# Chunked recurrence of the even layer: three chunk inverses side by side, a ring of half banks, a late norm in four spans

## The chip, the cores and the metric

The kernel runs on one core of a Trainium2 chip. The metric is the device time of one execution in microseconds: 2305.53 us, the median of three runs (2305.34 to 2306.35). One more execution was profiled; all rows below come from that one.

## The reference, cut to what matters

The kernel computes one step of a two-layer decoder trunk for 536 tokens: 16 meta tokens and 512 prompt tokens as one sequence, and 8 single sample tokens with states of their own. Each layer is a half SwiGLU block, a mixer, and a second half SwiGLU block. The change is in the mixer of the even layer, which runs HGRN2 heads (4) and RWKV-7 heads (8 of width 64) in parallel. RWKV-7 is a recurrence over tokens:

```
def rwkv7_scan(r, w, k, v, kk, a, s0):
    def step(s, inp):
        rt, wt, kt, vt, kkt, at = inp
        sa = jnp.einsum('bhij,bhj->bhi', s, -kkt)
        s = s * wt[:, :, None, :] + sa[..., None] * (kkt * at)[:, :, None, :] + vt[..., None] * kt[:, :, None, :]
        y = jnp.einsum('bhij,bhj->bhi', s, rt)
        return s, y
...
    mu = jnp.mean(y, axis=-1, keepdims=True)
    var = jnp.mean(jnp.square(y - mu), axis=-1, keepdims=True)
    yn = ((y - mu) * lax.rsqrt(var + RWKV_GN_EPS)).reshape(bsz, t, B_W) * prm['rwkv_ln_w'][e] + prm['rwkv_ln_b'][e]
    bonus = jnp.sum(r4 * k4 * prm['rwkv_rk'][e].reshape(B_HEADS, B_N), axis=-1, keepdims=True) * v4
    ob = (yn + bonus.reshape(bsz, t, B_W)) * g
    mix = jnp.concatenate([oa.astype(f32), ob], axis=-1).astype(h.dtype) @ prm['even_w_out'][e]
```

`oa` is the normalized output of the HGRN heads. The norm of `y` over each head, the bonus and the gate `g` are called the late norm here (`rpost`).

## The kernel before, in words

All activations lie transposed: 128 channels on the partitions, 536 tokens along the free dimension. Dense products run as three fp32r matmuls (high by high, high by low, low by high), in token parts of 272 and 264 columns (`PARTS`); a projection of 128 channels is 8 x 3 x 536 = 12,864 columns, and the program counts TensorE work in such columns.

The prompt's recurrence runs in chunks: one of 16 tokens and eight of 64, for two halves `d` of four heads each (two pairs of heads per half). That makes 18 chunks. For a chunk, `stage_g` (lines 1136 to 1172) spreads the rows over a block-diagonal tile, multiplies and transposes; then a unit triangular matrix is inverted by doubling, in up to five levels of two steps. `lev_t` (1175 to 1190) multiplies into `t1` (L1182), transposes the running inverse `xx` from the second level on (L1187), and ScalarE copies both out of PSUM (L1188, L1190). `lev_x` (1192 to 1206) multiplies again (L1204, L1198) and VectorE copies the result under a mask into `xx` (L1206, L1199). These 11 steps (7 for the short chunk) are a chain in which each step needs the one before. Five output steps follow, which also need the state of the chunk before: `st_p`, `st_t`, `st_sa`, `st_s`, `st_y` (1209 to 1264). All of them take PSUM from the ring `w`, four banks, one bank per request.

`waves` (1121 to 1302) puts these 280 steps into a list of slots: the two halves `d` are two chains, each chunk's inverse following that of the chunk before, and a chunk's output steps lie in the five slots behind its inverse. `even_mixer` (its loop is in the print below) calls one step after the other and puts filler between them. TensorE's queue is in the order in which the program is written (`manual_schedule`); the other engines are ordered by the framework's scheduler. After each step the loop adds `FILL` columns of credit, up to `FILL_MAX`, and spends it on `th_`: HGRN's projections (`proj_steps`, L240 to L242) and its heads' cores, `hcore` with `gla_core` and `gla_step` (scores L627, L638 and L618, factors L646, L657 on VectorE and L658 on GpSimd, state and output L669 to L713, sample states L724 to L752). Once these are used up it takes `mo`, the output projection of the first token part (`mix_out`), if two marks are set: "first" (HGRN's norm, `hgrn_norm`, is done) and "half" (the late norm has passed token 272).

Every `SAMPLE_EVERY`-th step advances `ts`, the sample's RWKV-7 step (`rsample`, four pairs of heads one after the other: transposes L1069, a trip through DRAM to broadcast the rows, products on GpSimd L1091 to L1115, reductions on VectorE L1094 and L1117). It works in the buffers `acc` and `sq`, of which there is one each; HGRN's norm and the late norm use the same two. Every `POST_EVERY`-th step advances `po`, which waits until head 3 of HGRN is projected and the recurrence has passed the end of the span, draws the rest of `ts`, lets HGRN's norm run if the heads are done, and then runs the late norm `rpost` over one span of tokens (`SPANS`) for two pairs of heads at a time. When the last step is issued, the loop issues what is left of `th_`, then of `po`, with `mo` between as the marks allow, then the rest of `mo`.

Of the kernel before, what the change touches and what calls it, by code (L numbers as in the profile page):

```python
# [63 lines left out]
LAG, LAG_LATER = 2, 3  # L64
SMALL_BLOCK = 32

HEAD_EVERY, ODD_FILL = 5, 4000
# [39 lines left out]
def trunk(ctx, tc, A, O):  # L107
    nc = tc.nc
# [15 lines left out]
    def psum(**sizes):  # L124
        if sizes == {tag: n for tag, (_, n) in rings.items()}:
            return
        banks.close()
        rings.clear()
        for tag, n in sizes.items():
            pool = banks.enter_context(tc.tile_pool(name=f"ps{tag}", bufs=n, space=bass.MemoryType.PSUM))  # L130
            rings[tag] = (pool, n)

    def bank(tag="m"):
        return til(rings[tag][0], [P, 512], tag)


    cf = til(cst, [P, CF_RM], "cf")
# [983 lines left out]
    def waves(pool, R):  # L1121
# [13 lines left out]

        def stage_g(d, ci, U):
            t0, n = CHUNKS[ci]
            na, nl = (2, 32) if n == 64 else (1, n)

            def both(z):  # L1140
                return z.rearrange("p (a h l) -> p a h l", a=2, h=2)[:, :na, :, :nl]

            U["xx"] = til(pool, [P, 2, 256], "xx", bufs=3)
            U["gm"] = til(pool, [P, 2, 320], "gm", bufs=3)
            nc.scalar.copy(U["xx"].rearrange("p u (v c) -> p (u v) c", v=2), ident.unsqueeze(1).to_broadcast([P, 4, P]))
            U["tm"] = til(pool, [P, 2, 384], "tm", bufs=3)
            if n < 64:
                nc.gpsimd.memset(U["gm"], 0.0)
            for i in range(2):
                Q = R[2 * d + i]  # L1150
                b_ = bd[i]
                for h in range(2):
                    hs = slice(64 * h, 64 * h + 64)
                    dst = b_[hs].rearrange("p (v a h l) -> p v a h l", v=4, a=2, h=2)[:, :, :na, h, :nl]
                    nc.vector.tensor_copy(dst, Q["sl"][hs, 0:4, t0:t0 + n].rearrange("p v (a l) -> p v a l", l=nl))
                g = bank("w")
                gv = g[:, 128:384].rearrange("p (v w t) -> p v w t", v=2, w=2)
                rhs = Q["sl"][:, 3:5, t0:t0 + n]
                nc.tensor.matmul(g[:, 0:128], b_[:, 384:512], b_[:, 0:128], start=True, stop=True)
                nc.tensor.matmul(gv[:, 0, :, :n], b_[:, 0:128], rhs, start=True, stop=True)  # L1160
                nc.tensor.matmul(gv[:, 1, :, :n], b_[:, 128:256], rhs, start=True, stop=True)
                one = g[:, 128:128 + n].rearrange("p (a l) -> p a l", l=nl)
                nc.vector.tensor_mul(both(U["gm"][:, i, 0:128]), one.unsqueeze(2).to_broadcast([P, na, 2, nl]),
                                     both(maskg[:, 0:128]))
                nc.vector.copy_predicated(U["xx"][:, i, 0:128], cu[:, CU_R:CU_R + 128], g[:, 0:128])
                nc.vector.tensor_mul(*(z.rearrange("p (v t) -> p v t", v=3)[:, :, :n]
                                       for z in (U["gm"][:, i, 128:320], g[:, 192:384], maskg[:, 128:320])))
                pt = bank("w")
                for v in range(3):
                    nc.tensor.transpose(pt[:, 128 * v:128 * v + 128], b_[:, 128 * v:128 * v + 128], ident)  # L1170
                nc.scalar.copy(U["tm"][:, i], pt[:, :384])
            nc.vector.copy_predicated(U["xx"][:, :, 128:256], lmask(0)[:, :, 128:256], U["gm"][:, :, 0:128])


        def lev_t(U, li):
            pt = bank("w")
            U["t1"] = til(pool, [P, 2, P], "t1", bufs=2)

            rs, cs = (slice(64, 128), slice(0, 64)) if li == 5 else (slice(0, 128), slice(0, 128))
            ks = cs  # L1180
            for i in range(2):
                nc.tensor.matmul(pt[rs, 128 * i:128 * i + cs.stop], U["gm"][ks, i, rs], U["xx"][ks, i, cs],  # L1182
                                 start=True, stop=True)
            if li > 1:
                px = bank("w")
                for i in range(2):
                    nc.tensor.transpose(px[:, 128 * i:128 * i + 128], U["xx"][:, i, 0:128], ident)  # L1187
            nc.scalar.copy(U["t1"][rs, :, cs], pt[rs, 0:256].rearrange("p (u c) -> p u c", u=2)[:, :, cs])  # L1188
            if li > 1:
                nc.scalar.copy(U["xx"][:, :, 128:256], px[:, 0:256].rearrange("p (u c) -> p u c", u=2))  # L1190
# [35 lines left out]
        def st_t(d, ci, U):  # L1226
            pt = bank("w")
            for i in range(2):
                nc.tensor.transpose(pt[:, 128 * i:128 * i + 128], pd[d][:, i], ident)
            U["pp"] = til(pool, [P, 2, P], "pp", bufs=2)  # L1230
            nc.scalar.copy(U["pp"], pt[:, 0:256].rearrange("p (u c) -> p u c", u=2))

        def st_sa(d, ci, U):
            ps = bank("w")
            for i in range(2):
                nc.tensor.matmul(ps[:, 128 * i:128 * i + 128], U["xx"][:, i, 128:256], U["pp"][:, i],
                                 start=True, stop=True)
            U["sa"] = til(pool, [P, 2, P], "sa", bufs=2)
            nc.scalar.copy(U["sa"], ps[:, 0:256].rearrange("p (u c) -> p u c", u=2))

        def st_s(d, ci, U):
# [52 lines left out]
        for d in range(2):  # L1294
            for i in range(2):
                p = 2 * d + i
                ps = bank("w")
                nc.tensor.transpose(ps[:, :P], S[d][:, i], ident)
                so = til(pool, [P, 64], "so", bufs=2)
# [393 lines left out]
```

## Time and profile before

| | |
|---|---|
| median of three runs | 2305.53 us |
| profiled execution, own time | 2313.27 us |
| profiled execution, span | 2311.5 us |
| mean granted TensorE clock | 0.991 of full speed |
| TensorE busy | 2256.8 us, 98% |
| VectorE busy | 1646.7 us, 71% |
| ScalarE busy | 1082.8 us, 47% |
| GpSimd busy | 143.5 us, 6% |
| HBM | 98 GB/s over the span |

PE is TensorE, DVE VectorE, ACT ScalarE, POOL GpSimd, SP the queue that issues most DMAs. Busy time counts an engine as busy while any of its instructions runs; matmuls overlap, so their single durations (about 0.28 us) are longer than the distance between their starts. An fp32 matmul of the recurrence shows as two records. The chunked recurrence runs from about 516 to 865 us of the span; the late norm's last span and the output projection follow.

### The profile page before, as it was taken

What the parts mean: (1) busy time and instruction counts of PE and PEld (TensorE: products, weight loads), DVE (VectorE), ACT (ScalarE), POOL (GpSimd) and SP (SyncE); (2) the same over time, 40 slices, a digit from 0 to 9 for tenths busy, and PEclk for the clock granted to TensorE, in tenths of its full rate; (3) what the DMA queues carried; (4) which work ended last, traced back from release to release, by engine and by line L of the source; (5) the groups of instructions that cost most, each with busy time, mean ns of one, the idle gap of its engine ahead of it and who ended that gap; (6) DMA issues with size and microseconds to landing.
All of it is one profiled execution on the core that took longest, in us unless ns stands there. A gap on an engine that the chain in (4) does not pass through costs nothing.

```text
span 2311.5 us, 47443 instructions
## 1 busy us (share of the span) xinstructions
PE 2256.8 (98%) x19520; PEld 2206.5 (95%) x19520; DVE 1646.7 (71%) x2971; ACT 1082.8 (47%) x2056; POOL 143.5 (6%) x192
## 2 busy tenths in 40 slices
PE   8999999999999999999999999999999999999998
PEld 8999999998998888999999999999999889999998
DVE  7858576686666878966757885857666777948576
ACT  6525254374444456434535452525434464525355
POOL 0000000312212100000000000000021210000000
PEclk9999999999999999999999999999999999999999
DMA  6323334223222116242423332333434353333324
GB/s 171 106 78 101 92 92 132 81 64 94 79 71 72 49 49 167 74 119 75 118 74 101 92 110 74 101 92 94 128 110 128 111 160 92 92 92 101 110 85 136
DMA packets 409393, 229.23 MB, mean 99 GB/s; under 512 B 19252, under 2 KB 400501, under 8 KB 409176
## 3 DMA queue, kind: packets, MB, share of 16 engines
q1 hardware_dynamic: 408456, 224.78, 33.5%
q8 instruction: 153, 2.51, 0.5%
q10 hardware_dynamic: 720, 1.42, 0.2%
q14 instruction: 64, 0.52, 0.1%
HBM read 211.19 MB, written 14.97 MB: 98 GB/s over the span
## 4 chain that ended last, share of the span: by engine, by line
PE 86%; DVE 5%; DMA 3%; ACT 2%; issue 1%; POOL 1%; SPq 0%; ACTq 0%; POOLq 0%; DVEq 0%
PE d L334 21%; PE d L335 21%; PE d L336 21%; PE d L240 5%; PE d L242 4%; PE d L241 4%; PE w L1182 1%; PE w L1204 1%; DMA vb<-dv 1%; DVE wlo L229 1%; DMA raw<-in_even_w_out_dram 1%; PE m L155 1%; DMA sq<-dr 1%; DMA raw<-in_odd_w_out_dram 1%; PE w L1187 1%
## 5 line engine op out<-in xcount | busy, mean ns | idle before, releaser
L240 PE MATMUL d<-hh,whi 128*128 128x264 f32 (+2 forms) x1136 | 343.6, 303 | 2.0 <-DVE xT L596 1.3
L242 PE MATMUL d<-hh,wlo 128*128 128x264 f32 (+2 forms) x1136 | 326.7, 288 | 1.9 <-DVE wlo L229 1.7
L241 PE MATMUL d<-hl,whi 128*128 128x264 f32 (+2 forms) x1136 | 326.6, 288 | 0.5 <-DVE hl L1418 0.5
L334 PE MATMUL d<-hh,whi 128*128 128x268 f32 (+1 forms) x832 | 237.8, 286 | 1.8 <-ACT hh L187 1.3
L335 PE MATMUL d<-hl,whi 128*128 128x268 f32 (+1 forms) x832 | 238.1, 286 | 0.9 <-DVE hl L188 0.9
L336 PE MATMUL d<-hh,wlo 128*128 128x268 f32 (+1 forms) x832 | 237.7, 286 | 0.7 <-DVE wlo L293 0.7
L240 PEld LDWEIGHTS d<-hh,whi 128*128 128x128 f32 x1136 | 216.1, 190 | 7.5 <-issue 2.4
L242 PEld LDWEIGHTS d<-hh,wlo 128*128 128x128 f32 x1136 | 215.4, 190 | 4.6 <-DVE wlo L229 4.0
L241 PEld LDWEIGHTS d<-hl,whi 128*128 128x128 f32 x1136 | 216.3, 190 | 0.9 <-DVE hl L1418 0.7
L534 DVE SCALAR_TENSOR_TENSOR xT<-d,xT 128x272 f32<-128x272 f32 (+2 forms) x192 | 82.9, 433 | 166.7 <-PE d L336 166.6
L334 PE MATMUL d<-hid,whi 128*128 128x264 f32 (+2 forms) x704 | 201.5, 287 | 0.0
L334 PE MATMUL d<-hid,whix 128*128 128x264 f32 (+2 forms) x704 | 201.2, 286 | 0.0
L335 PE MATMUL d<-hid,whix 128*128 128x264 f32 (+2 forms) x704 | 200.8, 285 | 0.0
L335 PE MATMUL d<-hid,whi 128*128 128x264 f32 (+2 forms) x704 | 200.7, 286 | 0.0
L336 PE MATMUL d<-hid,wlox 128*128 128x264 f32 (+2 forms) x704 | 200.6, 285 | 0.0
L336 PE MATMUL d<-hid,wlo 128*128 128x264 f32 (+2 forms) x704 | 200.5, 286 | 0.0
L334 PE MATMUL d<-sumh,whix 128*128 128x268 f32 (+1 forms) x576 | 170.9, 297 | 0.0
L336 PE MATMUL d<-sumh,wlo 128*128 128x268 f32 (+1 forms) x576 | 164.7, 286 | 0.0
L335 PE MATMUL d<-suml,whix 128*128 128x268 f32 (+1 forms) x576 | 164.4, 285 | 0.0
L334 PE MATMUL d<-sumh,whi 128*128 128x268 f32 (+1 forms) x576 | 164.2, 285 | 0.0
L336 PE MATMUL d<-sumh,wlox 128*128 128x268 f32 (+1 forms) x576 | 164.0, 285 | 0.0
L335 PE MATMUL d<-suml,whi 128*128 128x268 f32 (+1 forms) x576 | 164.0, 285 | 0.0
(383 smaller groups left out, 6557.8 us busy)
## 6 DMA issues: line engine op xcount, KB each, us to landing
raw<-in_ffn_gate_dram SPq DMA_DIRECT2D x44, 512.0 KB
raw<-in_ffn_up_dram SPq DMA_DIRECT2D x44, 512.0 KB
rawx<-in_ffn_gate_dram SPq DMA_DIRECT2D x44, 512.0 KB
rawx<-in_ffn_up_dram SPq DMA_DIRECT2D x44, 512.0 KB
raw<-in_ffn_down_dram SPq DMA_DIRECT2D x32, 512.0 KB
rawx<-in_ffn_down_dram SPq DMA_DIRECT2D x32, 512.0 KB
raw<-in_even_w_in_dram SPq DMA_DIRECT2D x30, 512.0 KB
raw<-in_odd_w_in_dram SPq DMA_DIRECT2D x25, 512.0 KB
```

What stands on the lines that cost most here:

```text
L155: nc.tensor.matmul(ps[:, :b - a], lhsT, rhs[:, a:b], start=True, stop=True)
L229: nc.vector.tensor_sub(lo[:, ks], raw[:, ks], hi[:, ks].bitcast(F32))
L240: nc.tensor.matmul(o, hi[:, k], h, start=(k == 0), stop=False)
L241: nc.tensor.matmul(o, hi[:, k], l, start=False, stop=False)
L242: nc.tensor.matmul(o, lo[:, k], h, start=False, stop=(k == nk - 1))
L334: nc.tensor.matmul(o, hi[:, k], rh(k), start=start and k == 0, stop=False, **kw)
L335: nc.tensor.matmul(o, hi[:, k], rl(k), start=False, stop=False, **kw)
L336: nc.tensor.matmul(o, lo[:, k], rh(k), start=False, stop=stop and k == nk - 1, **kw)
L534: nc.vector.scalar_tensor_tensor(xv[:, sl], ps, -0.5, xv[:, sl], ALU.mult, ALU.add)
L1182: nc.tensor.matmul(pt[rs, 128 * i:128 * i + cs.stop], U["gm"][ks, i, rs], U["xx"][ks, i, cs], start=True, stop=True)
L1187: nc.tensor.transpose(px[:, 128 * i:128 * i + 128], U["xx"][:, i, 0:128], ident)
L1204: nc.tensor.matmul(pd[:, i], lhsT, rhs, start=True, stop=True)
```

## The change

Five things change, all in the even layer.

- `waves` has `CHAINS` = 3 chains instead of two. The 18 chunks are dealt to whichever chain is free first, the halves `d` taking turns; a chain's steps are three slots apart, its start is staggered by four slots, and a chunk's output steps are two slots apart (`OUT_STEP`).
- The ring `w` still has four banks, but a request now gets half a bank of 256 columns (`halves`); two requests in a row share one bank. `stage_g` is cut to fit: its products take two halves, its transposes one and a half, and ScalarE copies them in two pieces.
- The late norm has four spans instead of three, since 272 columns don't fit a half bank.
- `FILL` is 550 instead of 1100, `SAMPLE_EVERY` 6 instead of 3, `POST_EVERY` 5 instead of 3.
- Buffer counts: `xx`, `gm`, `tm` 4 instead of 3, `t1` 3 instead of 2, `pp`, `sa` and `so` 1 instead of 2.

```diff
-FILL, FILL_MAX = 1100, 5000
+FILL, FILL_MAX = 550, 5000
...
-SAMPLE_EVERY, POST_EVERY = 3, 3
-SPANS = [0, 272, 400, 536]
-LAG, LAG_LATER = 2, 3
+SAMPLE_EVERY, POST_EVERY = 6, 5
+SPANS = [0, 144, 272, 400, 536]
+
+
+CHAINS, STAGGER, OUT_STEP = 3, 4, 2
...
     def bank(tag="m"):
-        return til(rings[tag][0], [P, 512], tag)
+        if tag != "w":
+            return til(rings[tag][0], [P, 512], tag)
+
+        if not halves:
+            t = til(rings[tag][0], [P, 512], tag)
+            halves.extend((t[:, 256:512], t[:, 0:256]))
+        return halves.pop()
...
-                g = bank("w")
-                gv = g[:, 128:384].rearrange("p (v w t) -> p v w t", v=2, w=2)
+                g, gl = bank("w"), bank("w")
+                gv = g.rearrange("p (v w t) -> p v w t", v=2, w=2)
...
+                nc.tensor.transpose(gl[:, 128:256], b_[:, 0:128], ident)
                 pt = bank("w")
-                for v in range(3):
-                    nc.tensor.transpose(pt[:, 128 * v:128 * v + 128], b_[:, 128 * v:128 * v + 128], ident)
-                nc.scalar.copy(U["tm"][:, i], pt[:, :384])
+                for v in range(2):
+                    nc.tensor.transpose(pt[:, 128 * v:128 * v + 128], b_[:, 128 * v + 128:128 * v + 256], ident)
+                nc.scalar.copy(U["tm"][:, i, 0:128], gl[:, 128:256])
+                nc.scalar.copy(U["tm"][:, i, 128:384], pt)
...
         slots = {}
-        for d in range(2):
-            t = LAG * d
-            for w in range(9):
-                U = {}
-                for fn in inverse(d, w, U):
-                    slots.setdefault(t, []).append((1 + d, fn, 0))
-                    t += 1
-                if w == 0 and d == 1:
-                    t += LAG_LATER
-                for i, st in enumerate((st_p, st_t, st_sa, st_s, st_y)):
-                    fn = lambda st=st, d=d, w=w, U=U: st(d, w, U)
-                    slots.setdefault(t + i, []).append((0, fn, int(i == 4)))
+        free = [STAGGER * i for i in range(CHAINS)]
+        after, ends = [0, 0], []
+        for c in range(18):
+            d, w, U = c % 2, c // 2, {}
+            k = free.index(min(free))
+            t = max(free[k], ends[c - CHAINS - 1] if c > CHAINS else 0)
+            for fn in inverse(d, w, U):
+                slots.setdefault(t, []).append((1 + k, fn, 0))
+                t += CHAINS
+            free[k] = t
+            t = max(t - CHAINS + 2, after[d])
+            for i, st in enumerate((st_p, st_t, st_sa, st_s, st_y)):
+                fn = lambda st=st, d=d, w=w, U=U: st(d, w, U)
+                slots.setdefault(t + OUT_STEP * i, []).append((0, fn, int(i == 4)))
+            after[d] = t + 4 * OUT_STEP
+            ends.append(after[d])
```

The order of instructions on TensorE, in the middle of the recurrence, with the semaphores that an instruction waits for. Before: two products of `lev_x` (L1204) of two chains, each with a ring tile `w` of its own, and three projection matmuls.

```order
L1204 MATMUL w_7519<-t_1124_7459,xx_7377 128x128 [waits Activation_49]
L1204 MATMUL w_7519<-t_1124_7459,xx_7377 128x128
L1204 MATMUL w_7523<-t_1126_7467,xx_7062 128x128 [waits Activation_49]
L1204 MATMUL w_7523<-t_1126_7467,xx_7062 128x128
L240 MATMUL d_7373<-hh_70,whi_7154 128x264
L241 MATMUL d_7373<-hl_71,whi_7154 128x264
L242 MATMUL d_7373<-hh_70,wlo_7155 128x264
```

After, the same step (now L1217) of two chains; both write the ring tile w_6679.

```order
L1217 MATMUL w_6679<-t_936_6652,xx_6420 128x128 [waits PE_49]
L1217 MATMUL w_6679<-t_936_6652,xx_6420 128x128
L251 MATMUL d_6462<-hh_70,whi_6130 128x264
L252 MATMUL d_6462<-hl_71,whi_6130 128x264
L253 MATMUL d_6462<-hh_70,wlo_6131 128x264
L1217 MATMUL w_6679<-t_938_6660,xx_6566 128x128 [waits DVE_49,Activation_49]
L1217 MATMUL w_6679<-t_938_6660,xx_6566 128x128
```

The end of the recurrence after the change: the four transposes of the last states (L1298 before, L1315 now) take two tiles, two transposes each, ahead of HGRN's scores.

```order
L251 MATMUL d_9234<-hh_70,whi_9227 128x272
L252 MATMUL d_9234<-hl_71,whi_9227 128x272
L253 MATMUL d_9234<-hh_70,wlo_9228 128x272
L1315 MATMUL w_9338<-cf_66,S_1430_9249 128x128 [waits PE_49]
L1315 MATMUL w_9338<-cf_66,S_1430_9249 128x128 [waits Activation_49]
L1315 MATMUL w_9349<-cf_66,S_1443_9324 128x128 [waits PE_49]
L1315 MATMUL w_9349<-cf_66,S_1443_9324 128x128 [waits Activation_49]
```

The second of the two transposes that share a tile now carries a wait for ScalarE, which copies the first one out.

TensorE again, the transposes and the state of HGRN's head 3. Before, they lie between chain steps (L1204, L1182, L1187, L1261) and the late norm (L155 on `w`).

```order
L155 MATMUL w_9869<-sl_616_4518,cf_66 128x272
L1204 MATMUL w_9873<-t_1624_9831,xx_9355 128x128 x2
L669 MATMUL m_9878<-cf_66,hk_8793 128x128 x4
L675 MATMUL m_9885<-cf_66,hv_9103 128x128 x4
L679 MATMUL m_9892<-cf_66,hk_8793 16x128
L681 MATMUL m_9892<-cf_66,hv_9103 16x128
L1182 MATMUL w_9896<-xx_9711,gm_9712 128x128 x2
L1187 MATMUL w_9900<-cf_66,xx_9711 128x128 x2
L688 MATMUL m_9906<-mtm_9891 128x128
L695 MATMUL m_9909<-vt_9884,ktm_9877 128x128 x4
L1261 MATMUL w_9923<-gm_9144,sa_9820 128x64 x2
L155 MATMUL w_9930<-lg_4507,g_604_4506 128x272
```

After, head 3's core stands behind the last step of the recurrence; here its last outputs (L723, L724), the transposes of the sample's last pair (L1080), the sum of HGRN's norm (L166 on `m`) and the first late norm (L166 on `w`).

```order
L724 MATMUL m_10068<-hq_9225,S_10058 128x128
L723 MATMUL m_10068<-acc_9807,vt_10035 128x128
L724 MATMUL m_10068<-hq_9225,S_10060 128x128
L1080 MATMUL m_10085<-cf_66,sl_616_4518 8x128
L1080 MATMUL m_10085<-cf_66,ws_618_4520 8x128
L1080 MATMUL m_10085<-cf_66,sl_616_4518 8x128 x2
L1080 MATMUL m_10094<-cf_66,sl_616_4518 8x128
L166 MATMUL m_10139<-acc_10127,cf_66 128x272
L166 MATMUL m_10143<-acc_10127,cf_66 128x264
L166 MATMUL w_10160<-sl_607_4509,cf_66 128x144
L166 MATMUL w_10160<-sl_610_4512,cf_66 128x144
L166 MATMUL w_10167<-acc_10159,cf_66 128x144
```

No chain step and no projection matmul stands between these any more.

## Rows read from the trace of the kernel before

**Rows 1.** Page: span, and busy time of TensorE with its share.

```profile
span 2311.5 us, 47443 instructions
PE 2256.8 (98%) x19520; PEld 2206.5 (95%) x19520; DVE 1646.7 (71%) x2971; ACT 1082.8 (47%) x2056; POOL 143.5 (6%) x192
```

**Rows 2.** Stretches: length, busy PE, PEld, DVE, ACT, POOL (counts), PEclk, DMA share, GB/s.

```profile
516.00:865.00 349.00, 329.73 (x3414) 308.04 (x3412) 245.39 (x709) 161.33 (x436) 71.45 (x78) 0.98 0.24 68
```

**Rows 3.** Waits of PE, 516 to 865: us in total, times, longest.

```profile
PE w L1182 <- DVE xx L1206: 2.3, 4, 0.9
```

**Rows 4.** Timeline of PE, projection matmuls: start, us, engine, instruction.

```profile
589.02 0.28 PE L240 MATMUL d<-hh,whi 128*128 128x272 f32 x1
589.15 0.29 PE L241 MATMUL d<-hl,whi 128*128 128x272 f32 x1
```

**Rows 5.** Timeline: level product, VectorE's copy, next product (idle before in brackets).

```profile
839.72 0.61 PE L1204 MATMUL w<-t,xx 128*128 128x128 f32 x4
840.53 0.38 DVE L1206 COPY_PREDICATED xx<-cu,w 128x256 f32<-128x256 uint8 x1
...
840.97 0.71 PE L1182 MATMUL w<-xx,gm 128*128 128x128 f32 x4 [0.64 <-DVE xx L1206]
```

**Rows 6.** Timeline: head 3 of HGRN, first, one level, last.

```profile
777.51 0.27 PE L724 MATMUL m<-cf,hv 128*8 128x128 f32 x1
...
781.13 0.46 PE L627 MATMUL m<-hq,hk 128*32 128x32 f32 x32
...
781.67 0.30 DVE L632 COPY_PREDICATED accd<-cu,m 128x128 f32<-128x128 uint8 x1
...
781.81 0.86 POOL L658 TENSOR_TENSOR hk<-hk,hf 128x264 f32<-128x264 f32 x1 [39.76 <-DVE xx L1206]
...
781.96 1.00 DVE L657 TENSOR_TENSOR hq<-hq,hf 128x264 f32<-128x264 f32 x1
...
816.39 0.39 PE L713 MATMUL m<-hq,S 128*128 128x128 f32 x2
```

**Rows 7.** Timeline: sample, second pair (first three) and last pair.

```profile
586.00 0.27 PE L1069 MATMUL m<-cf,sl 128*8 128x128 f32 x1
...
597.22 1.28 POOL L1091 TENSOR_TENSOR sq<-acc,sq 128x512 f32<-128x512 f32 x1 [33.65 <-DMA acc<-in_state_rwkv_dram]
...
625.95 0.69 DVE L1117 TENSOR_REDUCE sl<-sq 128x8 f32<-128x512 f32 x1 [2.79 <-POOL sq L1115]
...
716.36 1.47 POOL L1091 TENSOR_TENSOR sq<-acc,sq 128x512 f32<-128x512 f32 x1
...
740.78 1.27 POOL L1115 TENSOR_TENSOR sq<-acc,sq 128x512 f32<-128x512 f32 x1 [4.27 <-DMA sq<-dr]
```

**Rows 8.** Groups by line: HGRN's norm (829 to 848), late norm (865 to 890): busy, mean ns.

```profile
L179 ACT ACTIVATE sq<-oa 128x536 f32<-128x536 f32 x3 | 2.0, 651 | 0.1
...
L869 DVE SCALAR_TENSOR_TENSOR hl<-oa,vcol,hh 128x536 fp32r<-128x536 f32 x4 | 3.0, 773 | 0.0
L866 DVE TENSOR_TENSOR oa<-oa,rstd 128x536 f32<-128x536 f32 x4 | 2.7, 706 | 0.0
L180 DVE TENSOR_TENSOR acc<-acc,sq 128x536 f32<-128x536 f32 x3 | 2.1, 711 | 0.3 <-ACT sq L179 0.3
...
L166 DVE RECIPROCAL rstd<-rstd 128x272 f32<-128x272 f32 x1 | 1.9, 1852 | 0.1
...
L1319 DVE RECIPROCAL sl<-sl 128x136 f32<-128x136 f32 x4 | 3.7, 972 | 2.1 <-ACT sl L1317 2.1
...
L1314 DVE SCALAR_TENSOR_TENSOR acc<-w,sl 128x136 f32<-128x136 f32 x2 | 0.6, 289 | 0.0
```

**Rows 9.** Stretches around a fall of the clock, columns as in rows 2.

```profile
523.60:527.00 3.40, 1.62 (x41) 1.29 (x42) 3.35 (x15) 0.81 (x3) 0.00 (x0) 1.00 0.51 141
527.00:530.40 3.40, 2.94 (x44) 2.35 (x43) 2.44 (x8) 0.37 (x1) 0.86 (x1) 0.50 0.46 130
530.40:533.80 3.40, 3.40 (x18) 3.40 (x18) 1.23 (x5) 0.48 (x1) 1.23 (x2) 0.50 0.86 229
```

More of the change, by code (lines that the diff above doesn't have):

```diff
@@ L126, in psum @@
             return
+        halves.clear()
         banks.close()
@@ L131, in psum @@
             rings[tag] = (pool, n)
+    halves = []
     def bank(tag="m"):
-        return til(rings[tag][0], [P, 512], tag)
+        if tag != "w":
[4 more added lines that the diff above has]
+        return halves.pop()
     cf = til(cst, [P, CF_RM], "cf")
@@ L1141, in both @@
                 return z.rearrange("p (a h l) -> p a h l", a=2, h=2)[:, :na, :, :nl]
-            U["xx"] = til(pool, [P, 2, 256], "xx", bufs=3)
-            U["gm"] = til(pool, [P, 2, 320], "gm", bufs=3)
+            U["xx"] = til(pool, [P, 2, 256], "xx", bufs=CHAINS + 1)
+            U["gm"] = til(pool, [P, 2, 320], "gm", bufs=CHAINS + 1)
             nc.scalar.copy(U["xx"].rearrange("p u (v c) -> p (u v) c", v=2), ident.unsqueeze(1).to_broadcast([P, 4, P]))
-            U["tm"] = til(pool, [P, 2, 384], "tm", bufs=3)
+            U["tm"] = til(pool, [P, 2, 384], "tm", bufs=CHAINS + 1)
             if n < 64:
@@ L1155, in stage_g @@
                     nc.vector.tensor_copy(dst, Q["sl"][hs, 0:4, t0:t0 + n].rearrange("p v (a l) -> p v a l", l=nl))
-                g = bank("w")
-                gv = g[:, 128:384].rearrange("p (v w t) -> p v w t", v=2, w=2)
+                g, gl = bank("w"), bank("w")
+                gv = g.rearrange("p (v w t) -> p v w t", v=2, w=2)
                 rhs = Q["sl"][:, 3:5, t0:t0 + n]
-                nc.tensor.matmul(g[:, 0:128], b_[:, 384:512], b_[:, 0:128], start=True, stop=True)
+                nc.tensor.matmul(gl[:, 0:128], b_[:, 384:512], b_[:, 0:128], start=True, stop=True)
                 nc.tensor.matmul(gv[:, 0, :, :n], b_[:, 0:128], rhs, start=True, stop=True)
                 nc.tensor.matmul(gv[:, 1, :, :n], b_[:, 128:256], rhs, start=True, stop=True)
-                one = g[:, 128:128 + n].rearrange("p (a l) -> p a l", l=nl)
+                one = g[:, 0:n].rearrange("p (a l) -> p a l", l=nl)
                 nc.vector.tensor_mul(both(U["gm"][:, i, 0:128]), one.unsqueeze(2).to_broadcast([P, na, 2, nl]),
                                      both(maskg[:, 0:128]))
-                nc.vector.copy_predicated(U["xx"][:, i, 0:128], cu[:, CU_R:CU_R + 128], g[:, 0:128])
+                nc.vector.copy_predicated(U["xx"][:, i, 0:128], cu[:, CU_R:CU_R + 128], gl[:, 0:128])
                 nc.vector.tensor_mul(*(z.rearrange("p (v t) -> p v t", v=3)[:, :, :n]
-                                       for z in (U["gm"][:, i, 128:320], g[:, 192:384], maskg[:, 128:320])))
+                                       for z in (U["gm"][:, i, 128:320], g[:, 64:256], maskg[:, 128:320])))
+                nc.tensor.transpose(gl[:, 128:256], b_[:, 0:128], ident)
                 pt = bank("w")
-                for v in range(3):
-                    nc.tensor.transpose(pt[:, 128 * v:128 * v + 128], b_[:, 128 * v:128 * v + 128], ident)
-                nc.scalar.copy(U["tm"][:, i], pt[:, :384])
+                for v in range(2):
+                    nc.tensor.transpose(pt[:, 128 * v:128 * v + 128], b_[:, 128 * v + 128:128 * v + 256], ident)
+                nc.scalar.copy(U["tm"][:, i, 0:128], gl[:, 128:256])
+                nc.scalar.copy(U["tm"][:, i, 128:384], pt)
             nc.vector.copy_predicated(U["xx"][:, :, 128:256], lmask(0)[:, :, 128:256], U["gm"][:, :, 0:128])
@@ L1176, in lev_t @@
             pt = bank("w")
-            U["t1"] = til(pool, [P, 2, P], "t1", bufs=2)
+            U["t1"] = til(pool, [P, 2, P], "t1", bufs=CHAINS)
             rs, cs = (slice(64, 128), slice(0, 64)) if li == 5 else (slice(0, 128), slice(0, 128))
@@ L1298, in waves @@
                 nc.tensor.transpose(ps[:, :P], S[d][:, i], ident)
-                so = til(pool, [P, 64], "so", bufs=2)
+                so = til(pool, [P, 64], "so", bufs=1)
                 for h in range(2):
```

4 lines of the change are left out of this document (2 added, 2 removed).

## The prediction

> **What bounds the kernel now.** I read the totals first, then the busy time by stretch, then the waits of TensorE, then single instructions. TensorE is busy 98% of 2311.5 us [rows 1], so a change can give back only the time in which it stands, and costs whatever it makes it stand. The stage that the change rewrites, the chunked recurrence of the even layer with its fillers, runs from 516 to 865 us. In it TensorE is busy 329.73 of 349.00 us, VectorE 245.39, ScalarE 161.33, GpSimd 71.45 [rows 2]. TensorE is therefore the bound, and 19.3 us is all that it stands there. Its waits are scattered: the longest group by line is the level product that waits for VectorE's previous level, 2.3 us in 4 waits [rows 3]. What fills the gaps is projection work, whose matmuls of 264 to 272 columns follow each other every 0.12 to 0.13 us [rows 4]. Nothing in this stage is short of bandwidth, with DMA at a share of 0.24 [rows 2].
>
> **The change, part by part.** The sum is made against the profiled execution's own time, 2313.27 us (2311.5 of span and 1.8 around it), 7.7 us above the median of the runs, 2305.53; I take these 7.7 off at the end.
>
> *Three chains instead of two.* The 18 chunk inverses and their 90 output steps are the same instructions. Before, a step of a chain and its successor had one other chain, up to two output steps and filler between them. Afterwards they have two other chains, half an output step and less filler, so the distance in time is about the same. It can give back at most the 19.3 us, and I take 8, about the part of the recurrence in these waits (the rest waits in the HGRN core and for the sample): -8, bounds -19 and 0.
>
> *Half banks.* A ring entry is now half a PSUM bank, and consecutive requests share a bank. The program makes one bank one tile, and the order shows what it does with that. In the changed program the second `L1217` product on w_6679 waits for VectorE and ScalarE, and at the end of the stage each second `L1315` transpose waits for ScalarE, though it reads the same identity and the same state as the one ahead of it. So TensorE may not write the second half before the first has been copied out. Before, the two level products had two banks and waited only for their own operands. I counted 221 such tiles in the stage. In 133 the second half belongs to another step than the first, and in all 133 its first matmul carries a wait. In 53 nothing stands between the two on TensorE, in 16 one matmul (0.22 us), in 48 one trio of projection matmuls (3 x 0.12 = 0.37), in 16 more. The price of one round trip stands in the trace, where a level product waits for the copy of the last: product at 839.72, copy at 840.53 for 0.38, next product at 840.97 after 0.64 idle [rows 5]. Start to start this is 1.25 us for four matmul records that otherwise take 4 x 0.11 = 0.44, so 0.81 is lost. 53 x 0.81 + 16 x 0.59 + 48 x 0.44 + about 1 = 75. If the copies come late, because VectorE and ScalarE are busy 70% and 46% of the stage and a copy may queue behind one, 0.3 each is added, 115; if half of the waits fall into gaps that were there anyway, 35. I take 75, since the row is a wait of this very kind.
>
> The trace of before holds no bank with two users, so it can't say whether the wait could be left out. The Trainium skill, PSUM — Partial Sum Buffer, "PSUM bank collisions raise a hardware error", speaks against this part of the change: two engines may not touch the same bank and quadrant at once, even in different columns, and PSUM is to be guarded by bank, not by address. By that rule the 75 us stay; if guarding by address were enough they would be 0.
>
> *Less filler per step.* FILL falls from 1100 to 550 columns, and the number of steps stays 280. So the stage draws 154,000 columns of filler instead of 308,000. HGRN's 11 remaining projections (12,864 each) and its four cores (12 steps of 2500, the last of 1000) cost 243,500. Before they fit, with room for the late norm; now they don't. By the order 579 projection matmuls lay in the stage and 351 do afterwards. HGRN's head 2 is under way when the stage ends; head 3's core, the sample's last pair (SAMPLE_EVERY 6 instead of 3) and all of the late norm come after. There TensorE's order has nothing between them: the last `L724` of head 3, the sample's transposes `L1080`, the norm sum and the late norm's `L166` stand in a row, where before head 3's transposes had chain steps between them. TensorE's work is the same; what counts is the idle time.
> - Rest of head 2's core: some 9 steps with 6 to 9 projection matmuls (0.7 to 1.1 us) each, against a step of 2 to 2.5 us: 7 idle, bounds 3 and 12.
> - Head 3's core: 39 us before, from 777.51 to 816.78, beside other work [rows 6]. Alone, a level is 0.46 of scores, then 0.30 and up to 1.00 on VectorE beside 0.86 on GpSimd [rows 6], some 2.3 with the sample state's updates; with 7 us of transposes, state and output at the end, about 27, of which TensorE works 10: 17 idle, bounds 12 and 24.
> - The sample's last pair: a chain of DMA round trips and GpSimd products. The second pair took 586.00 to 626.64, 40.6 us; 11.2 of it up to the first product; the last pair's products and reduction took 26.4 from 716.36 (740.78 + 1.27 + 0.7 - 716.36) [rows 7]. 11 + 26 = 37, with 0.7 of TensorE in it: 36 idle, bounds 30 and 40. Nothing else can run: HGRN's norm and the late norm need the buffers acc and sq that it holds.
> - HGRN's norm up to where it frees acc: 4 squares of 0.65, 3 additions of 0.71, the sum [rows 8]: 6 idle, bounds 4 and 8.
> - The late norm of the first two spans, ahead of which the output projection may not start: two pairs each. On VectorE a pair is 2 x (0.97 + 7 x 0.29) = 6.0 [rows 8], four are 24, and HGRN's norm lays 2 x 1.8 + 4 x 0.71 + 4 x 0.77 = 9.5 between them [rows 8]. With some 4 of hand-overs 38, in which TensorE works 7: 31 idle, bounds 24 and 36.
> Together +97, bounds 73 and 120. Spans 3 and 4 lie beside the output projection, as span 3 did before.
>
> *Late norm in half banks.* In spans 3 and 4 there are 16 tiles whose second half waits in the same way, most behind nothing: 16 x 0.44 = 7, bounds 0 and 13. The fourth span's 16 more matmuls move no column more than before.
>
> *Other edits.* 36 more ScalarE copies, some 0.3 each, lie in ScalarE's idle half; if they were on the path they are within the late-copy bound above. The single buffers of pp, sa and so cost nothing while their readers are one step away.
>
> *Clock.* After a stretch in which TensorE was busy 1.62 of 3.40 us its granted clock was 0.50, that is 1.2 GHz, for the next 6.8 us [rows 9]. The tail will be in that state for long. Head 3's 10 us of TensorE grow, the rest hides in waits, and the first matmuls of the output projection pay some 2 us: +6, bounds 0 and 14.
>
> Sum: -8 + 75 + 97 + 7 + 6 = +177. 2313.27 + 177 = 2490.3, less 7.7 is 2482.5: I predict 2482 us.
>
> **The rivals.**
> 1. *The half-bank waits are hidden.* For: two other chains stand between a step and its successor, and the price row is one row. Against: the waits are on the neighbour in TensorE's own queue, not on the own chain, and 53 have nothing between. With 0 to 10 for them and 2 for the late norm: 2313.3 - 8 + 5 + 97 + 2 + 6 - 7.7 = 2408.
> 2. *Copies become the bound.* The 133 waits tie the three chains into one, so that each copy is needed at once and meets a busy VectorE (245 of 349 us [rows 2]) or ScalarE. Then each costs about 1.0 after filler: +133 instead of +75, 2540.
> 3. *Faster.* The four full banks are what the stage was short of; eight halves end its standing, and the late part is covered because VectorE, GpSimd and the DMA queue run ahead of TensorE there. It ends 19.3 us lower, at 2286. Against: the sample's transposes and head 3's core can't run ahead, since TensorE's own queue orders them. It decides if less than 19 us of the 97 show. The Trainium skill, Perfetto Trace Analysis, "Optimization Strategy", says that a gap that repeats on the saturated engine can mean too few PSUM buffers; here rows show only 2.3 us in the longest group.
> 4. *The change does less than it says*: the tail's idle time is smaller, since the DMA chain runs faster with the queues empty, and the stage gains its 19: 2313.3 - 19 + 40 + 73 + 0 + 4 - 7.7 = 2404, beside rival 1.
>
> **How the numbers follow.** My forecast 0.60, with its own range 2440 to 2525 (the bounds of the bank waits and the tail, not all at one end); rivals 1 and 4 0.22; rival 2 0.13; faster 0.03; and 0.02 that gains and losses meet within 0.2%, which is about what a measurement of this kernel can tell from no change. So faster 0.03, same 0.02, slower 0.95. The range that leaves out 2 in 10 is 2395 to 2550.
>
> **What would show it.** Right: waits of TensorE in the stage, on VectorE and ScalarE copies of the `w` tiles, of some 75 us together, in a stage about as long as before in spite of 228 projection matmuls less; after it a stretch of 30 to 40 us in which TensorE does almost nothing while GpSimd and the DMA queue work through the sample's last pair; a half clock there; VectorE dense before the output projection starts. Wrong: TensorE at over 95% in the stage (bank waits hidden), or sample work of the last pair ending before the recurrence does.

## The result, and the profile after

The changed kernel takes 2540.87 us, median of 4 runs (2536.77 to 2544.69). The kernel before, run beside it, takes 2305.94. The ratio is 1.1014, 95% interval 1.0992 to 1.1036: slower by 235 us. The profiled execution took 2539.71 us.

The page of the kernel after: the totals (to be read against [rows 1]), then busy tenths of TensorE and its granted clock in 40 equal slices of 63 us.

```profile
span 2537.9 us, 47630 instructions
PE 2338.9 (92%) x19552; PEld 2253.6 (89%) x19552; DVE 1663.0 (66%) x3007; ACT 1094.3 (43%) x2104; POOL 139.7 (6%) x192
...
PE   8999999987778883489999999999999999999998
...
PEclk9999999989999976599999999999999999999999
```

TensorE lost time in one place only, the 9th to the 18th slice. Its busy time also grew, by 82 us for 32 more matmuls: so part of the loss sits in the busy time, not in gaps. The mean granted clock of the whole execution is 0.957, where it was 0.991.

The same stretch by stages: the recurrence (516 to 917), rest of HGRN's head 2, the rest of a projection, head 3's core, the sample's last pair, HGRN's norm, late norm of spans 1 and 2, then spans 3 and 4 with the output projection. Columns as in [rows 2].

```profile
516.00:917.00 401.00, 316.82 (x2633) 272.74 (x2631) 178.95 (x535) 138.39 (x409) 46.71 (x54) 0.92 0.14 39
917.00:943.50 26.50, 25.99 (x277) 24.55 (x277) 12.28 (x35) 4.43 (x12) 4.15 (x6) 0.64 0.18 51
943.50:957.50 14.00, 14.00 (x116) 14.00 (x115) 8.76 (x22) 4.68 (x8) 0.00 (x0) 1.00 0.26 76
957.50:991.00 33.50, 18.73 (x287) 16.16 (x286) 15.08 (x40) 4.71 (x12) 7.54 (x11) 0.59 0.19 54
991.00:1027.00 36.00, 0.54 (x4) 0.09 (x1) 2.21 (x4) 1.44 (x3) 8.39 (x7) 0.54 0.38 113
1027.00:1033.40 6.40, 1.97 (x5) 1.53 (x6) 2.23 (x4) 3.76 (x6) 0.00 (x0) 0.50 0.00 0
1033.40:1067.00 33.60, 17.85 (x57) 13.31 (x56) 25.90 (x61) 9.78 (x26) 0.00 (x0) 0.50 0.00 1
1067.00:1149.70 82.70, 66.46 (x458) 61.43 (x456) 60.55 (x146) 38.25 (x82) 0.00 (x0) 0.93 0.42 115
```

The stretch of the recurrence is 52 us longer than the one of [rows 2] (which ends 4 us ahead of its last transposes; from the first product to the last transpose it is 398.0 against 348.9 us), although it holds 781 matmul records fewer. TensorE stands for 84.2 us in it, where it stood for 19.3. Between its end and the first FFN2 product lie 233 us (917.1 to 1149.7); before the two lay 49 us apart (869.3 to 918.1), in this stretch:

```profile
865.00:918.10 53.10, 49.97 (x392) 48.09 (x390) 40.83 (x91) 30.68 (x67) 0.00 (x0) 1.00 0.63 173
```

Waits of TensorE in the recurrence after, columns as in [rows 3]:

```profile
PE w L1179 <- DVE gm L1177: 20.2, 18, 2.4
PE w L1217 <- ACT py L1237: 7.9, 8, 1.8
PE w L1195 <- ACT xx L1203: 5.6, 15, 0.6
PE w L1315 <- ACT so L1318: 4.0, 2, 3.5
PE w L1249 <- ACT xx L1203: 3.3, 7, 0.5
PE w L1195 <- ACT pp L1244: 3.1, 6, 0.7
```

`L1217` computes a chain's level product. `py` is a copy that an output step makes of another tile and that the product doesn't read; what the two share is the bank. `L1195` waits for `xx`, `pp` and `sa` in the same way. The first row is one the prediction does not have: inside stage g one transpose writes into a bank that VectorE still reads. One case of each on the timeline (start, us, engine, instruction; idle before and its end in brackets):

```profile
856.08 0.38 PE L1228 MATMUL w<-gm,tm 128*128 128x128 f32 x2
856.30 0.39 PE L1230 MATMUL w<-sl,S 128*128 128x128 f32 x2
856.52 0.39 PE L1228 MATMUL w<-gm,tm 128*128 128x128 f32 x2
856.75 0.39 PE L1230 MATMUL w<-sl,S 128*128 128x128 f32 x2
...
857.17 0.26 ACT L1235 COPY pd<-w 64x128 f32<-64x128 f32 x1 [2.52 <-PE w L1230]
857.22 0.28 PE L253 MATMUL d<-hh,wlo 128*128 128x264 f32 x1
857.46 0.30 DVE L1235 COPY pd<-w 64x128 f32<-64x128 f32 x1 [1.10 <-ACT pd L1235]
857.79 0.27 ACT L1237 COPY py<-w 128x128 f32<-128x128 f32 x1 [0.36 <-DVE pd L1235]
858.11 0.71 PE L1217 MATMUL w<-t,xx 128*128 128x128 f32 x4 [0.61 <-ACT py L1237]
...
859.46 0.39 PE L1172 MATMUL w<-sl,bd 128*128 128x128 f32 x2
859.75 0.69 DVE L240 TENSOR_TENSOR wlo<-raw,whi 128x512 fp32r<-128x512 f32 x1
...
860.36 0.28 DVE L1174 TENSOR_TENSOR gm<-w,cf 128x128 f32<-128x128 f32 x1
860.56 0.29 DVE L1176 COPY_PREDICATED xx<-cu,w 128x128 f32<-128x128 uint8 x1
860.75 0.35 DVE L1177 TENSOR_TENSOR gm<-w,cf 128x192 f32<-128x192 f32 x1
...
861.16 0.33 PE L1179 MATMUL w<-cf,bd 128*128 128x128 f32 x1 [1.31 <-DVE gm L1177]
```

The first wait is three copies in turn, each 0.26 to 0.30 us, on engines that had stood for 2.52 and 1.10 us: neither was busy. The filler between the two users (its last matmul is the `L253`) was over at 857.50, and TensorE then stood for 0.61. In the second wait three reads of 0.28 to 0.35 by VectorE come after a filler piece, `L240`, in VectorE's own queue.

The row of `L1315` holds a term that the prediction put at nothing, the single buffer of `so`. At the end of the recurrence ScalarE's copy of each state waits until the DMA has taken the one before out of `so`, and the transpose that shares the bank waits for that copy:

```profile
914.13 0.42 ACT L1318 COPY so<-w 64x64 f32<-64x64 f32 x2 [1.55 <-DMA out_dram<-so]
916.13 0.43 ACT L1318 COPY so<-w 64x64 f32<-64x64 f32 x2 [1.57 <-DMA out_dram<-so]
916.61 0.48 PE L1315 MATMUL w<-cf,S 128*128 128x128 f32 x1 [3.53 <-ACT so L1318]
```

### The profile page after: what moved, and what is told of

The parts are those of the page before. It is cut to its first block, busy times and chain, and to the rows that moved or that the text cites. A ratio compares the mean times of both kernels' runs of the same rounds, so it can differ in the third digit from the quotient of the medians.

```text
span 2537.9 us, 47630 instructions
## 1 busy us (share of the span) xinstructions
PE 2338.9 (92%) x19552; PEld 2253.6 (89%) x19552; DVE 1663.0 (66%) x3007; ACT 1094.3 (43%) x2104; POOL 139.7 (6%) x192
## 5 line engine op out<-in xcount | busy, mean ns | idle before, releaser
L253 PE MATMUL d<-hh,wlo 128*128 128x264 f32 (+2 forms) x1136 | 330.4, 292 | 1.9 <-DVE wlo L240 1.7
L253 PEld LDWEIGHTS d<-hh,wlo 128*128 128x128 f32 x1136 | 219.6, 194 | 4.5 <-DVE wlo L240 3.8
```

What stands on the lines that cost most here:

```text
L253: nc.tensor.matmul(o, lo[:, k], h, start=False, stop=(k == nk - 1))
```

## The experiments

Each kernel ran beside the kernel before, on the same chip; "excess" is the difference of the two medians taken there, so chips don't mix. The changed kernel's own excess is 235.0 us. An interval is about 0.4% of the time wide, so a difference of two excesses is known to some 5 to 7 us.

**Whole banks.** The changed kernel with each `w` tile in a bank of its own:

```
-        if not halves:
-            t = til(rings[tag][0], [P, 512], tag)
-            halves.extend((t[:, 256:512], t[:, 0:256]))
-        return halves.pop()
+        return til(rings[tag][0], [P, 512], tag)[:, 0:256]
```

> The changed kernel with a whole bank per request again; chains, fillers and spans stay as changed. Theory (bank sharing makes TensorE wait for the copy of its neighbour's half): the recurrence took 401 us with 84 us of idle TensorE, about 106 us more than the work moved out of it would leave; nearly all of that goes, and some 8 us in the late norm: 2436 us, 2420 to 2455. Rival (the new order of the chains, with steps and output steps further apart, stretches the recurrence): only the late norm's 8 us go, 2530 us.

2422.13 us (2421.61 to 2425.23), ratio 1.0496 (1.0479 to 1.0514), excess 113.4: 121.6 us less than with half banks. The recurrence falls from 398 to 295 us, what follows it from 233 to 209. The theory holds.

**Old fillers.** The changed kernel, half banks kept:

```
-FILL, FILL_MAX = 550, 5000
+FILL, FILL_MAX = 1100, 5000
-SAMPLE_EVERY, POST_EVERY = 6, 5
+SAMPLE_EVERY, POST_EVERY = 3, 3
```

> The changed kernel with the old fillers: FILL 1100, SAMPLE_EVERY and POST_EVERY 3; half banks, three chains and four spans stay. Theory (what lies uncovered behind the recurrence costs): behind it the rest of head 2 took some 10 us more than its TensorE work, head 3 some 23, the sample's last pair 36, HGRN's norm 5, two spans of late norm 27, what follows some 20: about 120 us go, and the longer fillers cover a part of the bank waits: 2415 us, 2390 to 2440. Rival (in the recurrence these pieces wait just as long, because TensorE's queue orders them between bank waits): half or less of it goes, 2480 us or more.

2477.55 us (2468.62 to 2482.38), ratio 1.0728 (1.0703 to 1.0752), excess 168.8: only 66 us less. My number was wrong, the rival was near. What follows the recurrence does shrink from 233 to 72 us, but the recurrence grows from 398 to 489, and TensorE still stands for 96 of the 494 us of its stretch:

```profile
516.00:1010.00 494.00, 397.67 (x3421) 348.44 (x3419) 253.79 (x724) 170.44 (x485) 67.72 (x78) 0.87 0.18 49
```

Twice the filler did not remove the bank waits. Filler behind a waiting matmul stands in the same queue and waits with it; only filler between the two users of a bank covers the wait (the table further down). The late norm, now inside the recurrence, also draws halves: 178 tiles of the stage are shared by different steps in this run, where the kernel after has 141 (both counts with the two tiles of the last states), and in 89 of the 178 nothing stands between the two users.

**The sample early.** SAMPLE_EVERY alone goes back from 6 to 3.

> The changed kernel with SAMPLE_EVERY 3 instead of 6 alone: the sample's last pair is drawn within the recurrence. Theory (its DMA and GpSimd chain stood alone behind head 3 for 36 us): the 36 us go, 2505 us, 2498 to 2512. Rival (something else takes their place, such as late norm work that waits anyway, or the sample's products hold up HGRN's factors on GpSimd's queue in the recurrence): 2520 to 2541 us.

2498.91 us (2495.91 to 2508.77), ratio 1.0832 (1.0808 to 1.0856), excess 190.2: 45 us less, the recurrence unchanged (396 us), what follows 188 instead of 233. The theory holds; the 9 us beyond its 36 are little more than two excesses can differ by.

**The transpose first.** In stage g the transpose into `gl`'s second half goes ahead of VectorE's reads:

```
                 nc.tensor.matmul(gv[:, 1, :, :n], b_[:, 128:256], rhs, start=True, stop=True)
+                nc.tensor.transpose(gl[:, 128:256], b_[:, 0:128], ident)
...
-                nc.tensor.transpose(gl[:, 128:256], b_[:, 0:128], ident)
                 pt = bank("w")
```

> The changed kernel with one line moved: in the spreading step the transpose into the second half of the product's half bank is issued right behind that product, ahead of the three VectorE copies that read the bank. In the trace of the changed kernel TensorE waits there for VectorE's last copy, 20.2 us in 18 waits. Theory (a bank wait inside one step, which my prediction did not count): these 20 us go, 2520 us, 2515 to 2526. Rival (TensorE waits as long at the next bank, since the copies end no earlier): 2535 us or more.

2518.51 us (2514.07 to 2524.42), ratio 1.0911 (1.0892 to 1.093), excess 209.8: 25 us less, in the recurrence (374 us instead of 398). The theory holds.

**Halves shared within a step only.** Each step of the recurrence, each transpose of a last state (the expectation has these still share) and each group sum of the late norm starts with a new bank; the edit, cut:

```
             for _, fn, end in sorted(slots[t], key=lambda z: z[0]):
+                halves.clear()
                 fn()
+                halves.clear()
...
         def over(lhsT, rhs, fn):
+            halves.clear()
```

> The changed kernel, but each step begins with a new bank, so that the halves of one bank are shared only within one step (stage g's two or four halves, the last transposes); its ring then holds the same four banks. Theory (the cross-step waits are most of the cost of the half banks, those inside stage g some 20 us of it): about 2445, from 2425 to 2465. Rival (sharing inside a step is the main cost): 2490 or more, TensorE idle 70 us or more in the stage.

2433.43 us (2424.86 to 2437.27), ratio 1.0548 (1.0523 to 1.0572), excess 128.5: 106.5 us less. Its recurrence:

```profile
516.00:834.20 318.20, 280.99 (x2645) 259.50 (x2647) 180.07 (x536) 135.23 (x406) 47.14 (x54) 0.94 0.17 49
```

The idle time of TensorE falls from 84.2 to 37.2 us, and its busy time, for the same instructions (2633 and 2645 records seen), from 316.8 to 281.0. The busy time of the `w` tiles' instructions alone, the kernel after first, shows where that sits:

```profile
516.00:917.00 401.00, 250.63 (x1612) 203.89 (x1612) 80.89 (x264) 95.80 (x308) 0.92 0.14 39
```

```profile
516.00:834.20 318.20, 223.64 (x1612) 195.12 (x1612) 80.04 (x264) 93.50 (x304) 0.94 0.17 49
```

The same 1612 records take 27 us less. Two things are in this. The first is the clock: of the kernel after's 401 us some 66 are at 1.2 GHz, here some 37 of 318 (granted 0.92 and 0.94 in the mean). 173 of the records start at the lower clock there and 93 here; a record adds 0.25 to 0.26 us of busy time at the lower clock and 0.13 to 0.14 at the higher, so about 10 of the 27 us are the clock, an estimate from these figures. The second is overlap. A matmul that follows another at once overlaps it (856.08, 856.30, 856.52 above: pairs of records, 0.22 apart at 0.38 or 0.39 each), one that was held back doesn't. At the higher clock the records are about as long in both runs (280 and 275 ns in the mean), but each adds 0.143 us of busy time in the kernel after and 0.133 here.

The idle time can be read tile by tile. The slot list of the changed kernel gives the order in which the halves are asked for, and the 1612 records follow it one by one. In 139 tiles the halves belong to two steps. Sorted by what stands on TensorE between the two users, in the kernel after:

| between the two users | tiles | idle ahead of the second user, us | of them waited |
| --- | --- | --- | --- |
| nothing | 67 | 40.9, that is 0.61 each | 67 |
| one or two records | 6 | 1.9 | 4 |
| three projection matmuls | 48 | 8.9, that is 0.18 each | 23 |
| more | 18 | 0.9 | 2 |

Together that is 52.5 us. Ahead of the same 139 matmuls it is 0.8 us without the sharing. Ahead of `L1217` and `L1195` the trace shows no idle time of TensorE any more. What stays is `L1179`, as this theory has it. Its wait, then the rest of head 2 with the projection, and the late norm with the output projection:

```profile
PE w L1179 <- DVE gm L1177: 23.1, 18, 5.2
```

```profile
834.20:867.20 33.00, 32.34 (x390) 30.82 (x390) 20.80 (x56) 10.02 (x25) 4.25 (x6) 1.00 0.27 75
943.80:1045.20 101.40, 79.42 (x513) 73.79 (x512) 81.44 (x199) 44.55 (x103) 0.00 (x0) 0.82 0.33 92
```

**The fillers alone.** The kernel before with FILL 550, SAMPLE_EVERY 6 and POST_EVERY 5.

> The kernel before with the three filler numbers of the change alone (FILL 550, SAMPLE_EVERY 6, POST_EVERY 5); two chains, whole banks and three spans as before. Theory (the late part is caused by the filler numbers, whatever the chains and banks): about 2420, from 2400 to 2440, that is +97 to +130, with some 195 to 215 us between the end of the recurrence and the first FFN2 product instead of about 49. Rival (the late part comes about by the four spans or by three chains together with the fillers): 2340 or less.

2406.24 us (2404.55 to 2410.88), ratio 1.0445 (1.0427 to 1.0464), excess 101.3, with 202.6 us between the recurrence and the first FFN2 product. The theory holds, so neither the chains nor the banks make the late part. Its stretches: the recurrence, rest of head 2 and projection, head 3, the sample's last pair with HGRN's norm, late norm and output projection.

```profile
516.00:812.00 296.00, 271.58 (x2655) 254.77 (x2658) 175.89 (x533) 133.00 (x371) 47.62 (x54) 0.97 0.19 52
812.00:844.90 32.90, 32.22 (x389) 30.79 (x386) 20.72 (x56) 9.98 (x25) 4.00 (x6) 1.00 0.27 75
844.90:878.40 33.50, 18.69 (x283) 16.21 (x281) 15.33 (x39) 4.71 (x12) 7.51 (x11) 0.55 0.19 54
878.40:919.90 41.50, 1.30 (x8) 0.53 (x6) 4.58 (x7) 4.26 (x7) 8.39 (x7) 0.54 0.33 98
919.90:1014.50 94.60, 75.94 (x484) 67.53 (x485) 77.50 (x165) 42.22 (x89) 0.00 (x0) 0.87 0.35 98
```

**The chains with four spans.** The changed kernel with whole banks and the old fillers (the edits of the first two experiments together).

> The changed kernel with whole banks (its tiles are columns 0 to 255 of a bank of their own) and with the fillers of before (FILL 1100, SAMPLE_EVERY and POST_EVERY 3); the three chains and the four spans stay. Theory (bank waits and the late part are all the loss, the chains themselves give back at most the 19 us that TensorE stood): 2300, from 2290 to 2310, with a recurrence stage of about 345 us and TensorE idle 10 to 20 us in it. Rival A (the three chains and the four spans cost time of their own): 2325 to 2345, TensorE idle 40 us or more in the stage. Rival B (the two losses aren't independent and part of them stays): 2350 or more.

2340.71 us (2333.61 to 2343.29), ratio 1.0153 (1.0133 to 1.0173), excess 35.8. Wrong for the theory; by its time it is rival A, with TensorE idle for 35.5 us in the stage, where rival A wanted 40. So I took the rest apart.

**The chains with three spans.** As the last, with `SPANS = [0, 272, 400, 536]`.

> The kernel before with the three chains alone: whole banks, the fillers and the three spans of before. Theory: as with four spans or a little less, 2298, from 2288 to 2308; this is the term of the sum for the chains (-8, from -19 to 0) measured by itself. Rival (three chains cost time of their own, since four banks serve them all): 2320 or more.

2326.38 us (2320.35 to 2333.43), ratio 1.0097 (1.0076 to 1.0117), excess 21.5. The rival again, and one wait of TensorE in the recurrence stands out (`L1173` is the transpose into `gl` here):

```profile
PE w L1173 <- DVE xx L1170: 14.9, 15, 3.4
```

**The chains with the old stage g.** As the last, with the three transposes of stage g in one bank that nothing else uses:

```
-                nc.tensor.transpose(gl[:, 128:256], b_[:, 0:128], ident)
-                for v in range(2):
-                    nc.tensor.transpose(pt[:, 128 * v:128 * v + 128], b_[:, 128 * v + 128:128 * v + 256], ident)
+                for v in range(3):
+                    nc.tensor.transpose(pt[:, 128 * v:128 * v + 128], b_[:, 128 * v:128 * v + 128], ident)
```

> The three chains alone (whole banks, fillers and three spans of before), now also with stage g of before: its three transposes go to a bank of their own instead of one of them to the second half of the bank that VectorE still reads. Theory (the +21 of the chains alone is the wait of that transpose, 33.3 us in 33 waits in its trace, part of it given back elsewhere): 2303, from 2295 to 2312, no difference from before. Rival (three chains over four banks lose by themselves, the transpose's wait only stands where another would): 2318 or more.

(The 33.3 us there add the idle time of matmuls and of weight loads, which is nearly the same time twice. For the matmuls it is the 14.9 of the row.) 2313.98 us (2308.21 to 2323.95), ratio 1.0031 (1.0017 to 1.0045), excess 6.5: between the two, 2 us outside the theory's range. Stage g's transpose costs 15 of the 21.5. The chains, with their order and the changed buffer counts, which this run keeps, make the kernel a little slower, not faster; which of the three does it was not tried.

**The new stage g alone**, in the kernel before.

> The kernel before (two chains, whole banks, its fillers and spans) with stage g of the change alone: one transpose writes the second half of the bank whose first half VectorE still reads. Theory (the transpose waits for that copy, about 0.9 us each at 36 places, some of it given back): 2325, from 2315 to 2337, with 20 to 35 us of idle time of TensorE ahead of that transpose. Rival (with two chains VectorE is done sooner, or the stage has room): 2310 or less.

2324.31 us (2321.03 to 2333.12), ratio 1.008 (1.0058 to 1.0102), excess 16.8: the theory's time, and about the same cost beside two chains and whole banks as beside three. TensorE's idle time ahead of the transpose is below what I expected:

```profile
PE w L1168 <- DVE xx L1165: 13.3, 16, 2.0
```

**Four spans alone**, in the kernel before.

> The kernel before with four spans of the late norm instead of three, nothing else. Chains with four spans were 14 us slower than chains with three. Theory (the fourth span is work of its own and TensorE waits for VectorE at its tiles): 2317, from 2311 to 2325. Rival (four spans lose only beside three chains): 2308 or less.

2311.44 us (2307.82 to 2318.15), ratio 1.0018 (1.0005 to 1.0032), excess 4.0: at the lower end of the theory's range by the time, but nearer the rival by the excess. Beside three chains the same edit cost 14.3 (35.8 against 21.5). The traces don't bear that difference out: with the fourth span the first FFN2 product, which follows all the work that the edit touches, starts 4.0 us later beside three chains (947.2 against 943.2) and 5.0 later beside two (923.1 against 918.1), in one execution each. So the larger part of the 14.3 may be spread.

## Why the prediction was right, and which terms were not

The forecast was +177 us; it is +235. The time lies in the wide range, 9 us from its end, and above the forecast's own range of 2440 to 2525. Sign, place and both mechanisms were right, the size was short by 58. Of the signs, the waits on copies of `w` tiles and the late stretch came as described; the stage "about as long as before" did not, with 398.0 against 348.9 us. The runs form a staircase from the kernel after down to the one before (a step is known to some 5 to 7 us):

| step, by excess | measured | forecast |
| --- | --- | --- |
| halves shared by different steps, late norm and last states included (235.0 to 128.5) | 106.5 | 75 + 7 |
| halves shared within a step (128.5 to 113.4) | 15.1 | 0 |
| filler numbers (113.4 to 35.8) | 77.6 | 97 + 6, with the fourth span |
| fourth span (35.8 to 21.5) | 14.3 | in the above |
| stage g's transpose (21.5 to 6.5) | 15.0 | 0 |
| three chains, their order and buffer counts (6.5 to 0) | 6.5 | -8 |

*Half banks.* The mechanism is the one forecast: TensorE does not write one half until the other has been copied out. In the stage the sharing by different steps costs 83 us (398.0 against 314.7, the length from the recurrence's first product to its last transpose), against 75 from 133 tiles and the 0.81 of [rows 5]. The count was 6 short (139 by the slot list), so it is 0.60 a tile, where the forecast's mean was 0.56. That the two sums lie so near is in part luck. Neighbours stand for 0.61 us in the mean, near the 0.64 of [rows 5]; behind a trio of projection matmuls it is 0.18, well below the 0.44 that was taken there. All 139 have 52.5 us of idle time. Most of the rest is busy time: lost overlap, which the 0.81 holds in part, and time at the lower clock, which the forecast had in the tail alone. The late norm's halves were mis-sized: from its first group sum to the first FFN2 product 116.3 us pass in the kernel after (1033.4 to 1149.7) and 101.4 without the sharing, 15 where I had 7; the rest of head 2, after the stage, gains 7 more (25.9 against 18.5 us), and that is the clock: TensorE is busy throughout in both, at a granted 0.64 in the kernel after and 1.00 without the sharing. The Trainium skill, PSUM — Partial Sum Buffer, "PSUM bank collisions raise a hardware error", asks for these waits; the trace agrees that they stand in the program, and whether one could do without them was not tried.

*What I left out.* Of 221 tiles I priced the 133 that two steps share. The others were taken as free because one step fills both halves. That is the step that failed, though not for all of them. In 35 tiles (`lev_t`) both halves are written before either is read, and no idle time stands ahead of the second. In the 45 of stage g a reader stands between two writes. 15.1 us are the halves shared within a step, and 15.0 more are stage g's transpose, which stays when the banks are whole, since it goes into the tile that VectorE reads. The diff showed it: a transpose written behind three VectorE instructions, 36 times; all three read its bank in the 18 places where the two halves of its products share one, one of them does in the others. The single buffer of `so`, put at nothing too, has part in one wait of 3.5 us.

*The late part.* It came as described: 36 us in which TensorE works 0.54 while the sample's last pair runs alone (forecast 36 idle), then a norm at the half clock. By itself, in the kernel before, it costs 101.3 us, forecast 97 + 6. Beside the other edits it costs less, 77.6 with whole banks and 66.2 with half banks (235.0 less 168.8); why, no run shows. Inside the term two sizes were wrong against each other. TensorE's idle time after the recurrence is 74 us in that run (202.5 us of its last four rows, less 128.2 busy), not 97: late norm and head 2 left less of it. And its busy time in both stretches together is 20 us longer than before (399.7 over its five rows, against 329.7 [rows 2] and 50.0 in the row of 865 to 918.1), where I had 6 for the clock: head 3's core has 18.7 busy at a granted 0.55, where I had 10.

*The chains.* -8 was forecast, with bounds -19 and 0; it is +6.5. The 19.3 us that TensorE stood were not the chains' to give back: with three chains, whole banks and the old stage g it stands for 25.6 in a stage of 359.4.

```profile
516.00:875.40 359.40, 333.83 (x3442) 313.34 (x3440) 252.55 (x716) 164.18 (x443) 70.03 (x78) 0.97 0.25 69
```

*The rivals.* 1 (waits hidden) and 3 (faster) are refuted by 121.6 us for the banks. 4 has too little of both terms. Rival 2 named 2540, and that is the time, but not its mechanism: it wanted copies that meet a busy VectorE or ScalarE. They are busy 179 and 138 of 401 us in the stage, 45 and 35%, less than before (70 and 46%), and each cross-step tile costs 0.60, not 1.0. In the case on the timeline the two copying engines had stood for 2.52 and 1.10 us: there it is the latency of a round trip, not the copies' throughput. Of the 58 us 24 lie in the bank terms, which rival 2 has larger, and the others in terms that it doesn't contain.

No kernel run here beats the kernel before.

## What to carry to other kernels

Two users of one PSUM bank that are neighbours in TensorE's queue cost most of a round trip to the copying engine (here 0.61 us of idle time in the mean, in 67 of 67 cases, and lost overlap besides). Price every such pair, and inside one step those where a reader stands between two writes in the code itself. Filler covers such a wait only where it stands between the two users (0.18 us was left behind three projection matmuls); behind the waiting matmul it waits too, because the queue is in order. And before a filler budget is cut, add up what it has to hold: what no longer fits runs later with nothing beside it, here 101 us by three numbers.

## What I had not expected of the hardware

- A wait is dearer than its idle time. With 47 us less idle the stage became 83 us shorter; the other 36 were busy time of the same matmuls, part of it at the lower clock and part of it lost overlap.
- Half banks cost 121.6 us with the new fillers and 133.0 with the old (168.8 less 35.8), although the filler budget was twice as large in the second case. The fillers' own cost did not add up in this way: 101.3 alone, 77.6 and 66.2 beside the other edits.
- The clock fell inside the recurrence too where TensorE stood often: 0.87 in the run with the old fillers and half banks, 0.97 in the same stage with whole banks (the row below).

```profile
516.00:884.60 368.60, 333.09 (x3417) 308.27 (x3415) 245.38 (x718) 166.33 (x480) 68.90 (x78) 0.97 0.22 64
```
